# Products of a weight piece in another order in a hybrid decoder kernel: high halves first, remainders last

## The chip, the cores and the metric

The kernel runs on one core of a Trainium2 chip. The metric is the device time of one execution in microseconds (us), given as the median of several runs; less is better. The profile was taken on the chip in one further execution. Its engines are called PE (TensorE's matmuls; PEld is its weight loads), DVE (VectorE), ACT (ScalarE), POOL (GpSimd) and SP (SyncE, which issues most of the DMAs here).

## The reference

Two decoder layers over 256 tokens of width 2048, in float32. The first layer mixes tokens with latent attention, the second with a state-space scan; behind each mixer stands a dense MLP with a squared ReLU, and each part adds to the residual stream. The change lies in the MLP, which is computed twice:

```python
def squared_relu_mlp(h, w_in, w_out):
    u = jax.nn.relu(h @ w_in)
    return (u * u) @ w_out
...
        x = x + mix
        h = rms_norm(x, mlp_norm_g[i])
        x = x + squared_relu_mlp(h, mlp_w_in[i], mlp_w_out[i])
```

`w_in` is 2048 x 8192 and `w_out` 8192 x 2048, so each layer's MLP reads 134 MB of weights.

## The kernel before, in words

**Three products for one.** PE multiplies in a format with fewer bits than float32 (`F32R`). So each float32 operand is split in two: a high half, which is the value rounded to that format, and a remainder, which is the value less its high half. A product of `a` and `w` is summed from three: high a x high w, high a x remainder w, remainder a x high w. In the code the halves of the activations are `ah` and `al`, those of the weights `wh` and `wl`. The activations are the stationary operand (128 x 128, loaded by an instruction of its own, PEld), the weights the moving one (128 x 512). Each product is one matmul of 512 columns that adds to a PSUM bank.

**The flow of weights.** Weights come in units of 128 x 1024 float32, 512 KB. `Flow.next` (called at the head of `products` and, through `piece`, of `block`) keeps the flow ahead of PE: SP issues the DMAs of the units up to six ahead into the pool `raw` (6 buffers; some go to `rx`), and `convert` splits the units up to three ahead. The split of a unit is two instructions in `Flow.halves`: ACT copies the raw unit to its high half in a buffer of the pool `wh` (L102), then DVE subtracts that from the raw unit to give the remainder in a buffer of the pool `wl` (L103). Both pools have 4 buffers. A buffer can be written again when PE has run the last product that reads it.

**The MLP.** `mlp_body` walks over a list of tokens that `plan` writes out. A token is one unit of weights:

- `s` tokens belong to a scheme with seven block products in place of eight for `h @ w_in` (M1, N7, N5, N6, N4, M2, N3). Some of their units are sums of two pieces of weights, which DVE (L183) and DMAs that accumulate (POOL, L199) make. Such a unit goes to one PSUM bank (`st` in the trace, from the pools `acc` or `sm`) and has two halves of 512 columns, q = 0 and 1: six products.
- `c` tokens compute `h @ w_in` plainly (the first of eight column groups), `o` tokens `u @ w_out`. Their units go to two banks, one for each half of the tokens, t = 0 and 1: twelve products. An `o` block is four such units, 48 products, into the pair of banks of the pool `yp`; then `add_residual` (L436, DVE) adds first the bank t = 0 and then t = 1 to the residual stream. The next `o` block writes to the same pair of banks.

Between the blocks ACT and DVE evacuate the banks of the seven products (`after`: L620, L621 and others), and PE transposes the hidden values (L322, L324, to bank `sm`).

**The order of work.** PE runs its instructions in the order in which the program issues them (`manual_schedule`). In `products`, `self.flow.next(key)` stands first: what it issues on SP, ACT, DVE and POOL comes ahead of the unit's products. Lines L616 to L618 are the three products: L616 `ah x wh`, L617 `ah x wl`, L618 `al x wh`. The first `wl` product of a unit is its second product, and its last product reads `wh`.

**Where another order is in use.** `block` (L339, L340, L343), which computes the mixers' projections and the last part of each MLP, takes a unit in two passes: first all products with `wh` (L339 `ah`, L340 `al`, for both q and both t), then all with `wl` (L343).

Of the kernel before, what the change touches and what calls it, by code (L numbers as in the profile page):

```python
# [214 lines left out]
class Trunk:  # L215
# [343 lines left out]
    def mlp_body(self, mp, layer, gain):  # L559
        nc = self.nc  # L560
# [21 lines left out]
        def lhs_u(pp):  # L582
            return self.from_tiles([us[pp, 0], us[pp, 1]])
# [24 lines left out]

        def products(accs, key, lhs, kt, first, last):
            u, (h, lo) = self.flow.next(key)  # L610
            for q in range(2):
                k = 2 * kt + q
                wh, wl = h[:, q * 512:(q + 1) * 512], lo[:, q * 512:(q + 1) * 512]
                for t, b in enumerate(accs):
                    ah, al = lhs(k, t)
                    nc.tensor.matmul(b, ah, wh, start=first and q == 0, stop=False)  # L616
                    nc.tensor.matmul(b, ah, wl, start=False, stop=False)  # L617
                    nc.tensor.matmul(b, al, wh, start=False, stop=last and q == 1)  # L618

        sub = lambda o, a, b: nc.vector.tensor_tensor(o, a, b, ALU.subtract)  # L620
        plus = lambda o, a, b: nc.vector.tensor_tensor(o, a, b, ALU.add)  # L621
# [34 lines left out]
        for tok in tokens:  # L656
            key = (tok[0], layer) + tok[1:]
            if tok[0] == "s":
# [4 lines left out]
                if count.setdefault(name, 0) % 4 == 0:  # L663
                    pool = self.sm if name == "N7" else self.acc
                    bank[name] = pool.tile([P, 512], F32, tag=pool.name, name=self.name("st"))
                count[name] += 1
                products([bank[name]], key, lambda k, t: [x[:, k] for x in S[name]], d,
                         count[name] % 4 == 1, count[name] % 4 == 0)
                if count[name] % 4 == 0:
                    after(name, p)  # L670
                move(1.36)
            elif tok[0] == "c":
                _, p, j, o = tok
                if o == 0:
                    out["c"] = pair_of_banks(self.yp if j else self.acc)
                products(out["c"], key, lhs_x, o, o == 0, o == 7)
                if o == 7:
                    for t in range(2):
                        turn(relu(out["c"][t], t), p, j, t, TR[4])
                    if j:  # L680
                        when(3, steps[2])
                if o % 2:
                    self.tick()
                move(2.72)
            else:
                _, p, nb, o = tok
                if o == 0:
                    out[nb] = pair_of_banks(self.yp)
                products(out[nb], key, lhs_u(p), o, o == 0, o == 3)
                if o == 3:  # L690
                    self.add_residual(nb, out.pop(nb))
                move(2.72)
# [4 lines left out]
        for nb in range(4):  # L697
# [4 lines left out]
            accs = self.block(keys, lhs_u(7))  # L702
# [905 lines left out]
```

## Time and profile before

| | |
|---|---|
| median of 3 runs | 2285.71 us |
| lowest and highest run | 2285.32 and 2286.46 us |
| span of the profiled execution | 2284.5 us |
| first MLP, about | 272 to 970 us |
| second MLP, about | 1525 to 2270 us |
| products of L616 to L618 | 5424 |

The span runs from the first to the last instruction of the profiled execution; the time of a run has about 1.2 us more around it. In the profile, a line such as `L617 PE MATMUL st<-wl,xt ... x448 | 174.7, 390 | 0.0` is a group of instructions: line of the program, engine, operation, what it writes and reads by the program's names, how many, busy time in us, mean duration in ns, and the idle time of the engine just before them with what ended it. Matmuls are pipelined: one begins before the one ahead of it has ended, so busy times of PE are not a sum of steps. A row of the view of waits names the engine and line that waited, who ended the wait, the total in us, how many times, and the longest. A row of the timeline has the start and duration in us, engine, line, operation, tiles and count, and in brackets the idle time before it.

### The profile page before, as it was taken

To read this page: it belongs to the slowest core of one execution; us is meant where nothing else is said; L and a number is where in the kernel's file an instruction comes from. 1 tells how busy PE (TensorE), PEld (TensorE's weight loads), DVE (VectorE), ACT (ScalarE), POOL (GpSimd) and SP (SyncE) were. 2 spreads that over 40 slices of the span, in tenths; PEclk is the share of its full clock that TensorE was granted. 3 is DMA by queue.
4 is the path that set the end of the run, shared out by engine and by line. 5 is a ranking of instruction groups with operands and counts; after the bars stand their busy time and mean duration, and the time that the engine had idled before them with its cause. 6 is when DMAs were issued, how large, how long until landed. Compare 5 with 4: busy or idle time off the path is not lost.

```text
span 2284.5 us, 30768 instructions
## 1 busy us (share of the span) xinstructions
PE 2278.1 (100%) x10929; PEld 1889.6 (83%) x10929; DVE 1915.9 (84%) x2318; ACT 1390.1 (61%) x1947; POOL 275.5 (12%) x315
## 2 busy tenths in 40 slices
PE   9999999999999999999999999999999999999999
PEld 7898888888888888888888888888888888888887
DVE  7786698999898897687899688676989889989985
ACT  7775576566666666564666555545666666666663
POOL 1440000000000000100133213121000000000000
PEclk9999999999999999999999999999999999999999
DMA  8545678888888878667888787767688888888874
GB/s 315 173 153 159 211 230 267 259 255 270 264 255 259 267 232 271 227 208 241 277 280 278 245 275 264 229 222 229 204 265 248 259 270 253 260 275 247 267 232 160
DMA packets 167706, 557.16 MB, mean 244 GB/s; under 512 B 19040, under 2 KB 28192, under 8 KB 166528
## 3 DMA queue, kind: packets, MB, share of 16 engines
q1 hardware_dynamic: 151264, 502.44, 66.2%
q0 software_dynamic: 13888, 48.49, 10.0%
q10 hardware_dynamic: 2400, 4.27, 0.5%
q8 instruction: 86, 1.41, 0.3%
q14 instruction: 68, 0.56, 0.1%
HBM read 529.65 MB, written 6.41 MB: 235 GB/s over the span
## 4 chain that ended last, share of the span: by engine, by line
PE 96%; DVE 1%; DMA 1%; ACT 1%; issue 1%; POOL 0%; SPq 0%; ACTq 0%; DVEq 0%
PE acc L339 13%; PE acc L340 13%; PE acc L343 13%; PE yp L618 9%; PE yp L617 9%; PE yp L616 9%; PE st L617 7%; PE st L618 7%; PE st L616 7%; DMA wraw<-mi 1%; PE sm L324 1%; DVE wl L103 1%; PE y L1309 1%; PE sm L322 1%; PE acc L616 1%; PE acc L618 1%
## 5 line engine op out<-in xcount | busy, mean ns | idle before, releaser
L102 ACT ACTIVATE wh<-wraw 128x1024 fp32r<-128x1024 f32 (+1 forms) x818 | 856.2, 1053 | 570.4 <-PE acc L340 268.9
L103 DVE TENSOR_TENSOR wl<-wraw,wh 128x1024 fp32r<-128x1024 f32 (+1 forms) x818 | 985.5, 1221 | 240.6 <-ACT wh L102 216.6
L616 PE MATMUL yp<-wh,k 128*128 128x512 f32 x896 | 349.2, 390 | 0.0
L618 PE MATMUL yp<-wh,k 128*128 128x512 f32 x896 | 348.8, 389 | 0.0
L617 PE MATMUL yp<-wl,k 128*128 128x512 f32 x896 | 348.6, 389 | 0.0
L339 PE MATMUL acc<-wh,xt 128*128 128x512 f32 x704 | 279.7, 397 | 0.4 <-ACT wh L102 0.4
L340 PE MATMUL acc<-wh,xt 128*128 128x512 f32 x704 | 274.9, 390 | 0.1
L102 ACT ACTIVATE wh<-wrx 128x1024 fp32r<-128x1024 f32 x168 | 177.8, 1058 | 153.4 <-PE yp L618 101.7
L103 DVE TENSOR_TENSOR wl<-wrx,wh 128x1024 fp32r<-128x1024 f32 x168 | 204.3, 1221 | 36.6 <-ACT wh L102 35.6
L618 PEld LDWEIGHTS yp<-wh,k 128*128 128x128 f32 x896 | 168.2, 188 | 35.1
L617 PEld LDWEIGHTS yp<-wl,k 128*128 128x128 f32 x896 | 168.2, 188 | 34.9
L616 PEld LDWEIGHTS yp<-wh,k 128*128 128x128 f32 x896 | 168.2, 188 | 34.8
L339 PE MATMUL acc<-wh,k 128*128 128x512 f32 x496 | 196.5, 396 | 0.0
L340 PE MATMUL acc<-wh,k 128*128 128x512 f32 x496 | 193.3, 390 | 0.0
L343 PE MATMUL acc<-wl,xt 128*128 128x512 f32 x704 | 188.3, 389 | 0.0
L616 PE MATMUL st<-wh,xt 128*128 128x512 f32 x448 | 177.7, 397 | 0.0
L618 PE MATMUL st<-wh,xt 128*128 128x512 f32 x448 | 174.9, 390 | 0.0
L617 PE MATMUL st<-wl,xt 128*128 128x512 f32 x448 | 174.7, 390 | 0.0
L339 PEld LDWEIGHTS acc<-wh,xt 128*128 128x128 f32 x704 | 132.7, 188 | 29.4 <-ACT wh L102 1.6
L340 PEld LDWEIGHTS acc<-wh,xt 128*128 128x128 f32 x704 | 132.5, 188 | 28.5 <-issue 1.2
L343 PEld LDWEIGHTS acc<-wl,xt 128*128 128x128 f32 x704 | 132.1, 188 | 27.7
L199 POOL DMA_DIRECT2D wrx<-mi x56 | 49.2, 878 | 720.6 <-DVE wl L103 524.5
(318 smaller groups left out, 3527.0 us busy)
## 6 DMA issues: line engine op xcount, KB each, us to landing
wraw<-mi SPq DMA_DIRECT2D x256, 512.0 KB, 5.5
wraw<-mo SPq DMA_DIRECT2D x256, 512.0 KB, 5.6
wraw<-si SPq DMA_DIRECT2D x160, 512.0 KB, 5.2
wraw<-so SPq DMA_DIRECT2D x64, 512.0 KB, 5.2
wrx<-mi SPq DMA_DIRECT2D x56, 512.0 KB, 5.4
wrx<-mi POOLq DMA_DIRECT2D x56, 512.0 KB, 7.8
wraw<-wo SPq DMA_DIRECT2D x32, 512.0 KB, 4.0
taps<-xD SPq DMA_DIRECT2D x16, 768.0 KB, 8.4
```

Source lines behind the costliest of these rows:

```text
L102: self.last = nc.scalar.activation(h[:, v], raw[:, v], AF.Copy)
L103: self.last_lo = nc.vector.tensor_tensor(lo[:, v], raw[:, v], h[:, v].bitcast(F32), ALU.subtract)
L199: nc.gpsimd.dma_start(st["b11"].tile, quarter(d, 1, 0), accum_op=ALU.add)
L322: self.nc.tensor.transpose(b.bitcast(F32R)[:, v], words[:, v], self.ident_r)
L324: self.nc.tensor.transpose(b[:, v], src[:, v], self.ident)
L339: nc.tensor.matmul(accs[t][:, :n], ah, wh[:, q, :], start=first and kt + q == 0, stop=False)
L340: nc.tensor.matmul(accs[t][:, :n], al, wh[:, q, :], start=False, stop=False)
L343: nc.tensor.matmul(accs[t][:, :n], lhs(kt + q, t)[0], wl[:, q, :], start=False, stop=en and q == nk - 1)
L616: nc.tensor.matmul(b, ah, wh, start=first and q == 0, stop=False)
L617: nc.tensor.matmul(b, ah, wl, start=False, stop=False)
L618: nc.tensor.matmul(b, al, wh, start=False, stop=last and q == 1)
L1309: nc.tensor.matmul(y[t][c, o], part(t)[:, c], xg[g][t][:, o], start=True, stop=True)
```

## The change

Inside `products` the loops are parted. The old code ran for each half q and each bank t the three products L616, L617, L618 one after the other. The new code first runs, for both q and both t, the two products with the high half `h` of the weights, and then, in loops of their own, those with the remainder `lo`. The flags that open a bank's sum (`start`) stay with the first product of a bank; those that close it (`stop`) move from the last product with `al` to the last with `lo`. Nothing else is touched: the number of products, their operands, the flow's buffers, the tokens and their order stay.

```diff
         def products(accs, key, lhs, kt, first, last):
             u, (h, lo) = self.flow.next(key)
+            half = lambda w, q: w[:, q * 512:(q + 1) * 512]
             for q in range(2):
-                k = 2 * kt + q
-                wh, wl = h[:, q * 512:(q + 1) * 512], lo[:, q * 512:(q + 1) * 512]
                 for t, b in enumerate(accs):
-                    ah, al = lhs(k, t)
-                    nc.tensor.matmul(b, ah, wh, start=first and q == 0, stop=False)
-                    nc.tensor.matmul(b, ah, wl, start=False, stop=False)
-                    nc.tensor.matmul(b, al, wh, start=False, stop=last and q == 1)
+                    ah, al = lhs(2 * kt + q, t)
+                    nc.tensor.matmul(b, ah, half(h, q), start=first and q == 0, stop=False)
+                    nc.tensor.matmul(b, al, half(h, q), start=False, stop=False)
+            for q in range(2):
+                for t, b in enumerate(accs):
+                    nc.tensor.matmul(b, lhs(2 * kt + q, t)[0], half(lo, q), start=False, stop=last and q == 1)
```

For a unit with one bank the order of the six products changes from h, lo, h, h, lo, h to h, h, h, h, lo, lo. For a unit with two banks the twelve go from (h, lo, h) four times, three to a bank, to eight with h, two to a bank in turn, and then four with lo, one to a bank in turn.

## The prediction

> **What bounds the kernel now.** I read the page's head and its chain of waits first, to find the engine whose time is the span.
>
> ```profile
> span 2284.5 us, 30768 instructions
> ...
> PE 2278.1 (100%) x10929; PEld 1889.6 (83%) x10929; DVE 1915.9 (84%) x2318; ACT 1390.1 (61%) x1947; POOL 275.5 (12%) x315
> ...
> PEclk9999999999999999999999999999999999999999
> ...
> PE 96%; DVE 1%; DMA 1%; ACT 1%; issue 1%; POOL 0%; SPq 0%; ACTq 0%; DVEq 0%
> ```
>
> The chain that ended last is 96% PE, and the granted clock never falls. So the time is a sum of products, and a change of order can only gain where PE stands still. Next I asked who made PE wait. A product is a weight load (PEld) and a matmul (PE); where the load waits for data, PE stands. The view of waits, for the loads, from the start of the first MLP to the end of the second (columns: us in all, times, longest):
>
> ```profile
> PEld st L617 <- DVE wl L103: 3.2, 8, 0.5
> ...
> PEld yp L617 <- DVE wl L103: 0.5, 2, 0.3
> ```
>
> Ten times L617, the product with the remainder `wl`, waited for VectorE to make it, 3.7 us together. L616 and L618, the products with the high half `wh`, have no row. This is the only idle time that the changed lines have to give: 0.16% of the span. What a wait costs is read from the steps from one start to the next in PE's timeline. First undisturbed ones, from a `block` of the second mixer:
>
> ```profile
> 1303.08 1.07 PE L343 MATMUL acc<-wl,xt 128*128 128x512 f32 x4
> 1303.98 0.39 PE L339 MATMUL acc<-wh,xt 128*128 128x512 f32 x1
> ...
> 1306.70 0.39 PE L339 MATMUL acc<-wh,xt 128*128 128x512 f32 x1
> ```
>
> From 1303.98 to 1306.70 run the twelve products of one piece: 2.72 us, a step of 0.227, while each "lasts" 0.39, since a product overlaps the next. Now the longest of the ten waits:
>
> ```profile
> 569.32 0.39 PE L618 MATMUL st<-wh,sN 128*128 128x512 f32 x1
> 569.55 0.40 PE L616 MATMUL st<-wh,sN 128*128 128x512 f32 x1
> 570.01 0.50 PE L617 MATMUL st<-wl,sN 128*128 128x512 f32 x1
> 570.35 0.40 PE L618 MATMUL st<-wh,sN 128*128 128x512 f32 x1
> ```
>
> From 569.55 to 570.35 two steps took 0.80 us instead of 0.454: this wait of 0.50 cost 0.35. The 0.15 between them is what a load can be late without delaying the product before it.
>
> **The change part by part.** It keeps the number of products and sorts them. A one-bank unit (bank `st`) has six; the old order is, for each half-piece q, high, remainder, high; the new one four with `wh`, then two with `wl`. A two-bank unit (blocks "c" and "o") has twelve; new: eight with `wh`, then four with `wl`. The groups by line give the counts:
>
> ```profile
> L617 PE MATMUL yp<-wl,k 128*128 128x512 f32 x896 | 348.6, 389 | 0.0
> ...
> L343 PE MATMUL acc<-wl,xt 128*128 128x512 f32 x704 | 188.3, 389 | 0.0
> ...
> L617 PE MATMUL st<-wl,xt 128*128 128x512 f32 x448 | 174.7, 390 | 0.0
> ...
> L617 PE MATMUL st<-wl,sN 128*128 128x512 f32 x336 | 131.5, 391 | 0.3
> ...
> L617 PE MATMUL yp<-wl,xt 128*128 128x512 f32 x64 | 25.1, 392 | 0.0
> ...
> L617 PE MATMUL acc<-wl,xt 128*128 128x512 f32 x64 | 24.9, 389 | 0.0
> ```
>
> 1808 remainder products move: 784 in one-bank units and 1024 in two-bank units. No instruction is added or removed; every other queue gets its work as before, since `flow.next`, which issues conversions and loads, stands ahead of the products in both orders.
>
> *The products themselves: 0.* The old order used one stationary operand twice running (`ah` with `wh`, then with `wl`); the new one doesn't. That loses no saved load: the page counts 10929 loads for 10929 products. The new order of a two-bank unit is already run by `block` (L339, L340, then L343), so its speed can be read off the timeline above: four remainder products that alternate between two banks took 0.90 us, from 1303.08 to 1303.98, four plain steps. The groups agree: 389 ns for L343, 389 to 392 for L617. Rounding of these means leaves ±0.5 ns on each of the 1024 products that now alternate: ±0.5 us. I take 0.
>
> [...]
>
> *The ten waits: minus 2.2 us.* Each costs its idle time less the 0.15 that a load has to spare: 3.7 - 10 x 0.15 = 2.2 us. In the new order the first `wl` product is three steps later in a one-bank unit (0.68 us) and seven later in a two-bank unit (1.59 us). The longest wait was 0.50, so each of the ten is covered. In the unit shown, which starts at 569.55, the remainder would be wanted at 569.55 + 4 x 0.227 = 570.46; it was ready at 570.01. What is late next: nothing that has a row. The units behind start up to 0.35 us earlier, and their own remainders are wanted 0.68 to 1.59 us later than now.
>
> *Release of the buffers: 0.* The last `wh` product moves from the 6th to the 4th place, or from the 12th to the 8th: its buffer comes free 0.45 or 0.91 us earlier. The last `wl` product moves from the 5th to the 6th, or 11th to 12th: 0.23 us later. Who waits for these buffers, in the whole kernel:
>
> ```profile
> ACT wh L102 <- PE yp L618: 260.3, 172, 1.7
> DVE wl L103 <- ACT wh L102: 252.2, 247, 3.7
> ...
> ACT wh L102 <- PE st L618: 71.0, 250, 0.3
> ```
>
> ACT waits for the last high product of a unit (L618) and VectorE for ACT; VectorE has no row in which it waits for a remainder's buffer. Both would therefore run earlier. PE doesn't wait for them except the ten times above, so this is cover, not time.
>
> *Evacuation of the first bank: 0, covered.* In a two-bank unit the first bank's last product moves from the 9th to the 11th place, 0.45 us later; the second bank's stays last. Its reader at the end of an "o" block is `add_residual` on VectorE (L436):
>
> ```profile
> 761.11 0.39 PE L617 MATMUL yp<-wl,k 128*128 128x512 f32 x1
> ...
> 761.27 1.28 DVE L436 TENSOR_TENSOR x<-yp,x 128x512 f32<-128x512 f32 x2
> 761.33 0.39 PE L618 MATMUL yp<-wh,k 128*128 128x512 f32 x1
> ...
> 761.76 1.06 ACT L102 ACTIVATE wh<-wraw 128x1024 fp32r<-128x1024 f32 x1 [1.66 <-PE yp L618]
> ...
> 763.57 1.23 DVE L183 TENSOR_TENSOR wraw<-wraw,wraw 128x1024 f32<-128x1024 f32 x1 [1.01 <-DMA wraw<-mi]
> ...
> 764.28 0.39 PE L616 MATMUL yp<-wh,k 128*128 128x512 f32 x1
> ```
>
> The first add began at 761.27, while the block's last product, of the other bank, began at 761.33. Now the first bank ends with the product in the slot of 761.11, at 761.50; ACT started 0.04 after the product it waited for, so the add starts at about 761.54, 0.27 us late. Queued behind it are the second add and VectorE's next piece. Here both fit: VectorE idled 1.01 us after them, and the bank's next writer starts at 764.28. If that cover were gone, it would cost 0.27 us for each block (second rival). The "c" blocks' `relu` on ACT shifts likewise, but there are only two a layer. The row of 761.76 also shows what hides the later release of `wl`: between the release of the high buffer and VectorE's use of the other stands ACT's conversion, 1.06 us.
>
> Sum: -2.2 us. The profiled execution spans 2284.5, 1.2 under the median of the runs, 2285.7 (what lies around the span); the same difference on both sides gives a span of 2282.3 and a time of **2283.5 us**, -0.1%.
>
> **The rivals.**
>
> *The waits stay.* VectorE's lateness may be more than the ten waits show, and the waits move to the new `wl` place. For it: VectorE is the engine with least room. Stretches of the two MLPs:
>
> ```profile
> 272.00:970.00 698.00, 697.83 (x3168) 576.22 (x3167) 616.69 (x615) 437.94 (x487) 45.47 (x67) 1.00 0.82 254
> 1525.00:2270.00 745.00, 744.90 (x3429) 614.74 (x3428) 645.24 (x642) 456.65 (x504) 50.04 (x67) 1.00 0.80 246
> ```
>
> (columns: length, then busy time of PE, PEld, DVE, ACT, POOL.) VectorE is busy 88% and 87%. Against it: it has 81 and 100 us free, and the longest wait is 0.50 against 0.68 of new room. Time: 2285.7.
>
> *VectorE pays for the later bank (the other side).* Place: L436 behind each "o" block. Price 0.27 us a block:
>
> ```profile
> L436 DVE TENSOR_TENSOR x<-yp,x x112: 679/682/687, 352.8 to 2237.2; 128x512 f32<-128x512 f32 x112
> ```
>
> 112 adds are 56 blocks, so at most 56 x 0.27 = 15.1 us, with the ten waits unremoved: 2300.8. It decides where the work behind the add has less than 0.27 us to spare even after its remainder's later place. For it: the 88%. Against it: the 1.01 us of idle in the block shown, and the 0.68 to 1.59 us that the pieces gain.
>
> *The step behind a transpose shrinks too (faster).* Where a unit follows a transpose, its first step is long:
>
> ```profile
> 568.02 0.30 PE L324 MATMUL sm<-ident,s 128*128 128x128 f32 x1
> ...
> 568.08 0.48 PE L616 MATMUL st<-wh,sN 128*128 128x512 f32 x1
> ...
> 568.39 0.40 PE L617 MATMUL st<-wl,sN 128*128 128x512 f32 x1
> ```
>
> 0.31 instead of 0.227. If this were the second product's wait for `wl`, the new order would end it. The transposes to bank `sm` bound their number:
>
> ```profile
> L324 PE MATMUL sm<-ident,s 128*128 128x128 f32 x167 | 33.7, 281 | 0.0
> L322 PE MATMUL sm<-ident,tr 128*128 128x128 f32 x229 | 26.9, 236 | 0.0
> ```
>
> Four to a group, at most 99 places, 0.083 us each: 8.2 us, with the ten waits 2275.3. Against it: the `block` order has the same long step behind short products:
>
> ```profile
> 1301.13 0.50 PE L339 MATMUL acc<-wh,xt 128*128 128x512 f32 x1
> 1301.47 0.39 PE L340 MATMUL acc<-wh,xt 128*128 128x512 f32 x1
> ```
>
> [...]
>
> **How the numbers follow.** The forecast has 0.78; the waits stay 0.10; the transposes 0.04; VectorE pays 0.06; the banks 0.02. A measurement of this kernel can tell about 0.2% from no change, 4.6 us: 2281.1 to 2290.3 is "the same". Forecast and first rival lie inside: same 0.88, faster 0.04, slower 0.08. Range: below, the whole 3.7 us of idle is gained instead of 2.2, with the runs' scatter (2285.32, 0.4 under the median) and the 0.5 of rounding: 2281.1. Above, nothing is gained, with the scatter on that side (2286.46, 0.75) and the 0.5: 2287.0. The rivals outside it hold 0.12.
>
> **What would show it.** Right: no row of a load waiting for `wl` within the MLPs; four high products, then two (or eight, then four) at 0.227 us a step; PE's busy time as now; ACT's waits for PE's high products end earlier. Wrong: a row of L436 waiting for PE together with a new wait of PE (second rival); a granted clock below 1.00, or remainder products over 0.227 us apart (banks); short steps behind transposes. The forecast would also fail if VectorE or ACT ran their instructions in another order than now.

## The result, and the profile after

| | before | after |
|---|---|---|
| median | 2285.71 us | 2303.01 us |
| lowest and highest | 2285.32 and 2286.46 us | 2300.80 and 2305.64 us |
| profiled execution | span 2284.5 us | 2305.32 us, span 2303.5 us |

The ratio of after to before is 1.0077, with an interval of 1.0065 to 1.009: the kernel is 0.8% slower, 17 us, where 2.2 us less were forecast. Of the kernels in the experiments below, e1 and e6 had one run each, of 6050 and 3260 us, far off all others; these two are left out of the ratios. The change shifted the lines behind it: the products are now L615 (`ah x wh`), L616 (`al x wh`) and L619 (`ah x wl`), while L103, L183 and L436 are as before.

The head of the page of after:

```profile
span 2303.5 us, 31032 instructions
...
PE 2284.5 (99%) x10929; PEld 1891.2 (82%) x10929; DVE 1914.7 (83%) x2318; ACT 1389.4 (60%) x1947; POOL 275.2 (12%) x315
```

Each engine's count of busy instructions is the same as before (the 264 more in the head are of kinds that the page doesn't count as busy), and so is DVE's busy time (1914.7 against 1915.9). PE is 19 us short of the span now; before it was 6.4 short. So no engine got more work: PE stands still. For whom, the view of waits tells (us in all, times, longest):

```profile
DVE wraw L183 <- DMA wraw<-mi: 37.1, 18, 4.5
...
DVE x L436 <- PE yp L619: 15.7, 28, 1.1
...
PE yp L615 <- DVE x L436: 11.5, 9, 3.0
```

Before, PE had no row in which it waited for L436, and the first row read:

```profile
DVE wraw L183 <- DMA wraw<-mi: 18.1, 27, 2.0
```

PE waits for `add_residual`, the add that empties its bank. And L183, the sum that makes the unit N7 from two raw pieces, waits longer for the DMA of its second piece, although the same DMAs are issued. The view of waits for the weight loads, from the start of the first MLP to the end of the second, still shows what the forecast was about:

```profile
PEld yp L615 <- ACT wh L102: 4.3, 3, 1.6
...
PEld st L619 <- DVE wl L103: 0.8, 2, 0.5
```

Of the ten waits for the remainder `wl`, 3.7 us together, two with 0.8 us are left. That gain is there, and something larger stands on top of it. The first row is a part of that: its three loads stand ahead of the first product of a block, where PE waits for L436. ACT had been done for 0.2 to 0.5 us when these loads began (at the first it ended at 515.25, the load began at 515.63), so the add ended these waits too.

**One block in both traces.** DVE's timeline of before at the end of an "o" block (start, duration, engine, line, tiles, count, idle time ahead):

```profile
676.54 1.23 DVE L103 TENSOR_TENSOR wl<-wraw,wh 128x1024 fp32r<-128x1024 f32 x1
677.68 1.28 DVE L436 TENSOR_TENSOR x<-yp,x 128x512 f32<-128x512 f32 x2
679.41 1.23 DVE L183 TENSOR_TENSOR wraw<-wraw,wraw 128x1024 f32<-128x1024 f32 x1 [0.44 <-DMA wraw<-mi]
```

The two adds come first, then the sum, which waits 0.44 us for its DMA with nothing urgent behind it. The same place after:

```profile
678.85 1.23 DVE L103 TENSOR_TENSOR wl<-wraw,wh 128x1024 fp32r<-128x1024 f32 x1
684.56 1.23 DVE L183 TENSOR_TENSOR wraw<-wraw,wraw 128x1024 f32<-128x1024 f32 x1 [4.48 <-DMA wraw<-mi]
685.70 1.28 DVE L436 TENSOR_TENSOR x<-yp,x 128x512 f32<-128x512 f32 x2
686.90 2.35 DVE L103 TENSOR_TENSOR wl<-wraw,wh 128x1024 fp32r<-128x1024 f32 x2
```

The sum now stands ahead of the adds. DVE runs its queue in order, as the rows show: for 4.48 us it waits for the DMA while two full banks wait for it. Not all of the 4.48 comes from the swap. The two adds take 1.2 us, by which the sum now comes earlier; but the DMA too took longer here, 7.8 us from issue to landing (676.66 to 684.44) against 5.5 before (673.76 to 679.28). Why it did, no run here shows. PE's timeline there:

```profile
682.95 0.61 PE L619 MATMUL st<-wl,sN 128*128 128x512 f32 x2
686.53 0.47 PE L615 MATMUL yp<-wh,k 128*128 128x512 f32 x1 [2.97 <-DVE x L436]
...
687.48 0.63 PE L616 MATMUL yp<-wh,k 128*128 128x512 f32 x1
687.91 0.63 PE L615 MATMUL yp<-wh,k 128*128 128x512 f32 x1
688.33 0.63 PE L616 MATMUL yp<-wh,k 128*128 128x512 f32 x1
```

The next "o" block's first product starts 0.83 us behind the start of the adds. A microsecond later the steps are 0.42 to 0.43 us instead of 0.227, and the granted clock is lower: 0.61 from 686.40 to 690.40, against 1.00 in the stretch before. The windows of both (length, busy time of PE, PEld, DVE, ACT and POOL with counts, granted clock, share of the DMA engines, GB/s):

```profile
683.00:686.40 3.40, 0.56 (x3) 0.14 (x1) 1.84 (x3) 1.06 (x1) 0.00 (x0) 1.00 1.01 278
686.40:690.40 4.00, 3.87 (x10) 2.96 (x11) 4.00 (x5) 0.55 (x1) 0.00 (x0) 0.61 0.54 133
```

**Who moved the sum.** In the program's text nothing on DVE changed place. But only PE's order is written out by hand; DVE's and ACT's queues are ordered when the program is compiled. The instruction order of the two compiled programs can be compared, buffer by buffer: 157 of DVE's 2318 instructions and 95 of ACT's stand elsewhere, none of SP's or POOL's. DVE's order at one block, before:

```
L103 wl_4368
L436 x_142<-yp_4246
L436 x_146<-yp_4247
L183 wraw_4399<-wraw_4397,wraw_4399
L103 wl_4388
```

and after:

```
L103 wl_4368
L183 wraw_4399<-wraw_4397,wraw_4399
L436 x_142<-yp_4246
L436 x_146<-yp_4247
L103 wl_4388
```

At ten "o" blocks, five in each MLP, each the first block of its pair of columns, the sum for N7 moved ahead of both adds in this way. At these ten the sum waited 9.0 us for its DMA before and 26.8 after.

**The account.** From the trace one can take, for each 512-column product in the two MLPs, the step from its start to the next start, less the plain 0.2267 us, and add these up. It gives 12.3 us before and 31.2 us after: 18.9 more, against 19.0 more of span. Of the 31.2, the pauses ahead of the ten blocks are 13.2 us (one of 3.13, two of 2.1 to 2.5, three of 1.0 to 1.4, four of 0.2 to 0.7), and 22 products behind three of them, at a granted clock of 0.50 and steps of about 0.427 us, 22 x 0.2 = 4.4 us. The other steps hold 13.6 us, 1.3 more than before: about 1.6 less in waits for `wl` (2.2 before, 0.5 after), about 3 more in small ones. 1.8 of these 3 are steps of 0.30 to 0.34 us at the head of the ten blocks, two or three behind each pause.

### The profile page after: what moved, and what is told of

The parts are those of the page before. It is cut to its first block, busy times and chain, and to the rows that moved or that the text cites. A ratio compares the mean times of both kernels' runs of the same rounds, so it can differ in the third digit from the quotient of the medians.

```text
span 2303.5 us, 31032 instructions
## 1 busy us (share of the span) xinstructions
PE 2284.5 (99%) x10929; PEld 1891.2 (82%) x10929; DVE 1914.7 (83%) x2318; ACT 1389.4 (60%) x1947; POOL 275.2 (12%) x315
## 4 chain that ended last, share of the span: by engine, by line
PE 95%; DVE 2%; DMA 2%; issue 1%; ACT 0%; POOL 0%; DVEq 0%; SPq 0%; ACTq 0%
PE acc L339 13%; PE acc L340 13%; PE acc L343 13%; PE yp L615 9%; PE yp L619 9%; PE yp L616 9%; PE st L615 7%; PE st L619 7%; PE st L616 7%; DMA wraw<-mi 1%; DVE wl L103 1%; PE sm L324 1%; PE sm L322 1%; PE y L1310 1%; PE acc L615 1%
## 5 line engine op out<-in xcount | busy, mean ns | idle before, releaser
L103 DVE TENSOR_TENSOR wl<-wraw,wh 128x1024 fp32r<-128x1024 f32 (+1 forms) x818 | 984.8, 1222 | 236.9 <-ACT wh L102 218.9
L615 PE MATMUL yp<-wh,k 128*128 128x512 f32 x896 | 352.4, 393 | 11.6 <-DVE x L436 11.5
L616 PE MATMUL yp<-wh,k 128*128 128x512 f32 x896 | 350.7, 391 | 0.0
L619 PE MATMUL yp<-wl,k 128*128 128x512 f32 x896 | 241.7, 392 | 0.0
L103 DVE TENSOR_TENSOR wl<-wrx,wh 128x1024 fp32r<-128x1024 f32 x168 | 204.5, 1222 | 25.6 <-ACT wh L102 24.5
L615 PEld LDWEIGHTS yp<-wh,k 128*128 128x128 f32 x896 | 169.1, 189 | 52.6 <-issue 11.3
L619 PEld LDWEIGHTS yp<-wl,k 128*128 128x128 f32 x896 | 169.8, 190 | 35.8
L616 PEld LDWEIGHTS yp<-wh,k 128*128 128x128 f32 x896 | 169.1, 189 | 34.5
L343 PE MATMUL acc<-wl,xt 128*128 128x512 f32 x704 | 188.3, 389 | 0.0
L615 PE MATMUL st<-wh,xt 128*128 128x512 f32 x448 | 177.7, 397 | 0.0
L616 PE MATMUL st<-wh,xt 128*128 128x512 f32 x448 | 174.8, 390 | 0.0
L343 PEld LDWEIGHTS acc<-wl,xt 128*128 128x128 f32 x704 | 132.1, 188 | 27.7
L619 PE MATMUL st<-wl,xt 128*128 128x512 f32 x448 | 138.1, 389 | 0.0
```

Source lines behind the costliest of these rows:

```text
L103: self.last_lo = nc.vector.tensor_tensor(lo[:, v], raw[:, v], h[:, v].bitcast(F32), ALU.subtract)
L343: nc.tensor.matmul(accs[t][:, :n], lhs(kt + q, t)[0], wl[:, q, :], start=False, stop=en and q == nk - 1)
L615: nc.tensor.matmul(b, ah, half(h, q), start=first and q == 0, stop=False)
L616: nc.tensor.matmul(b, al, half(h, q), start=False, stop=False)
L619: nc.tensor.matmul(b, lhs(2 * kt + q, t)[0], half(lo, q), start=False, stop=last and q == 1)
```

## The experiments

The theory to be tested: the loss is the ten swaps in DVE's queue, and without them the change brings what was forecast. Its rivals: the later end of the first bank costs by itself, the new product order does (banks in turn), or only one kind of unit is to blame. Times are medians; the ratios are to the kernel before on the same chip, 2286.65 us for the first four kernels and 2286.30 us on another chip for the last three. The last column is the sum of steps over 0.2267 us as above.

| kernel | median, us | ratio, interval | span of the profile | steps over 0.2267 |
|---|---|---|---|---|
| before (first profile) | 2285.71 | | 2284.5 | 12.3 |
| after (first profile) | 2303.01 | 1.0077, 1.0065 to 1.009 | 2303.5 | 31.2 |
| e1: after, sum held behind the adds | 2284.10 | 0.999, 0.998 to 0.9999 | 2282.3 | 10.1 |
| e2: old products, sum first | 2301.08 | 1.0067, 1.005 to 1.0084 | 2300.0 | 28.0 |
| e3: new order in one-bank units only | 2297.62 | 1.0046, 1.0031 to 1.0061 | 2296.4 | 23.8 |
| e4: new order in two-bank units only | 2304.29 | 1.0079, 1.0064 to 1.0094 | 2303.0 | 31.1 |
| e6: e3, sum held | 2285.67 | 0.9999, 0.9989 to 1.0008 | 2285.6 | 11.5 |
| e7: e4, sum held | 2286.20 | 1.0, 0.999 to 1.0009 | 2283.4 | 11.2 |
| e8: after, all sums held | 2284.81 | 0.9995, 0.9986 to 1.0005 | 2282.8 | 10.9 |

### e1: the changed kernel with the sum held behind the adds

The products stay as changed. `add_residual` keeps its last add, and N7's sum is told to be issued behind it:

```diff
             if name == "N7":
-                add("b22", "b12", "b22")
+                with flow.tc.issue_after(flow.add.ins) if flow.add else nullcontext():
+                    add("b22", "b12", "b22")
...
-            self.nc.vector.tensor_tensor(x, accs[t], x, ALU.add)
+            self.flow.add = self.nc.vector.tensor_tensor(x, accs[t], x, ALU.add)
```

> The new product order, with one thing held: the sum for N7 (L183, b22) may not stand ahead of the add_residual (L436) that the program wrote before it, in VectorE's queue. Theory A (the ten places where that sum, which waits for its DMA, went ahead of the two adds cost the time): PE's waits of up to 3.0 us for the bank of an 'o' block vanish, no product runs at the 0.427 us step behind them, and the time is 2282 to 2286 us. Theory B (the new product order itself, or the rest of the moved work on VectorE and ACT, costs it): the time stays at 2300 or above. Between 2287 and 2299: both have a share, to be read as the difference from 2284 and from 2303.

Measured: 2284.10 us, 19 us less than after, and 2.55 under the kernel before on the same chip, with an interval that just excludes no change. It is faster than both kernels, than the one before by little. ACT's order is that of after, so ACT's 95 moved instructions cost nothing by themselves.

DVE's timeline at the block that was shown above (L104 makes the remainders here, L184 is the sum, L438 the adds, L618, L619 and L622 the products):

```profile
675.77 1.23 DVE L104 TENSOR_TENSOR wl<-wraw,wh 128x1024 fp32r<-128x1024 f32 x1
677.57 1.29 DVE L438 TENSOR_TENSOR x<-yp,x 128x512 f32<-128x512 f32 x2 [0.58 <-PE yp L622]
678.78 2.35 DVE L104 TENSOR_TENSOR wl<-wraw,wh 128x1024 fp32r<-128x1024 f32 x2
...
682.30 1.22 DVE L184 TENSOR_TENSOR wraw<-wraw,wraw 128x1024 f32<-128x1024 f32 x1
```

The adds run as soon as the bank is full, and the sum, now behind three remainders as well, finds its data there and waits for nothing. The view of waits agrees:

```profile
DVE x L438 <- PE yp L622: 22.8, 40, 1.1
...
DVE wraw L184 <- DMA wraw<-mi: 3.3, 4, 1.1
```

The first row is the later end of the first bank: 40 times DVE waits for it, 0.57 us each. PE has no row for L438 at all. So that lateness is real and costs nothing.

### e2: the old products with the sum first

The kernel before, in which ten sums, those at the ten blocks, are put ahead of the adds by an order between them; ten DVE rows stand elsewhere than before, no row of ACT.

```diff
-                add("b22", "b12", "b22")
+                total = add("b22", "b12", "b22")
+                if p in range(2, 7) and flow.adds and flow.done - flow.adds[0] <= 4:
+                    for ins in flow.adds[1:]:
+                        flow.tc.add_manual_dep(ins, total.ins.name, mybir.DependencyInfo(
+                            mybir.DependencyClass.NoSync, mybir.DependencyReason.DATA), reason="sum first")
...
-            self.nc.vector.tensor_tensor(x, accs[t], x, ALU.add)
+            ins = self.nc.vector.tensor_tensor(x, accs[t], x, ALU.add).ins
+            self.flow.adds = ([self.flow.done] if t == 0 else self.flow.adds) + [ins] if nb == 0 else None
```

> The old product order, with ten instructions moved in VectorE's queue: at the same ten 'o' blocks the sum for N7 (L183) is put ahead of the two adds. Theory A: the loss comes back without any change of the products: waits of PE for the bank at these ten blocks, 2297 to 2306 us. Theory B (product order): 2285 to 2287 us.

Measured: 2301.08 us. No product has moved against the kernel before, and most of the loss is there: 15.7 us of steps over 0.2267, against 18.9 after. From its view of waits and from its DVE timeline (L442 are the adds, L624 the products `ah x wh`):

```profile
PE yp L624 <- DVE x L442: 10.4, 9, 2.3
```

```profile
510.37 1.23 DVE L104 TENSOR_TENSOR wl<-wraw,wh 128x1024 fp32r<-128x1024 f32 x1
514.98 1.23 DVE L184 TENSOR_TENSOR wraw<-wraw,wraw 128x1024 f32<-128x1024 f32 x1 [3.38 <-DMA wraw<-mi]
516.12 1.28 DVE L442 TENSOR_TENSOR x<-yp,x 128x512 f32<-128x512 f32 x2
```

It is the picture of after: the sum waits for its DMA, the adds behind it, PE behind the adds. The ten swaps alone bring most of the loss, and with them taken out (e1) nothing of it is left.

### e3 and e4: the new order in one kind of unit only

In e3 units with one bank run the new loops and those with two banks the old ones; in e4 it is the other way round.

```diff
             u, (h, lo) = self.flow.next(key)
+            if len(accs) == 1:
...
+            else:
...
```

> The new order in the six-product units (one bank) alone, the old one in the twelve-product units. VectorE's queue then has the sum ahead of the adds at two of the ten blocks (the second 'o' block group of the second column pair in each layer), which cost 0.5 and 0.6 us in the changed kernel. Theory A: eight of the ten waits for a remainder are gone (-1.9 us) and about 1 us is lost at the two blocks: 2284 to 2287 us. Theory B: the 1568 moved products of these units cost their share, about 784 of 1808 of 17 us: about 2293 us.

> The new order in the twelve-product units (two banks) alone, the old one in the six-product units. VectorE's queue has the sum ahead of the adds at all ten blocks. Theory A: nearly the whole loss, 2297 to 2306 us, with waits of PE for the bank at the ten blocks. Theory B: the share of these units, about 1024 of 1808 of 17 us: about 2295 us.

e3 was expected near the kernel before and took 2297.62 us: a miss. Its order on DVE explains it. At two of the ten blocks the sum stands ahead of both adds, at the other eight between the two. DVE's timeline at one of the eight, and the row of waits:

```profile
513.45 0.69 DVE L436 TENSOR_TENSOR x<-yp,x 128x512 f32<-128x512 f32 x1 [0.17 <-PE yp L629]
516.55 1.23 DVE L183 TENSOR_TENSOR wraw<-wraw,wraw 128x1024 f32<-128x1024 f32 x1 [2.40 <-DMA wraw<-mi]
517.69 0.68 DVE L436 TENSOR_TENSOR x<-yp,x 128x512 f32<-128x512 f32 x1
```

```profile
PE yp L627 <- DVE x L436: 7.2, 9, 1.2
```

The first add escapes and PE can start the next block with the first bank; it stops at the second. Each pause is shorter, 1.2 us at most, and the loss is 11.5 us of steps. So even the part of the change that leaves the "o" blocks' own products alone reorders DVE around them.

e4 took 2304.29 us, like after. All ten pauses stand ahead of a block's first product:

```profile
PE yp L616 <- DVE x L436: 13.0, 10, 2.1
```

### e6 and e7: the same two, with the sum held

e6 is e3 and e7 is e4, each with the edit of e1.

> The kernel with the new order in the six-product units alone, now with the sum for N7 held behind both adds. Theory A (where the sum stands among the adds is the whole loss; in the kernel without the hold it stood between the two adds at eight blocks and ahead of both at two): the 11 us go, and of the ten waits for a remainder the eight in these units go too: 2283.5 to 2286 us. Theory B (the new order of these units costs time by itself): it stays above 2290 us.

> The kernel with the new order in the twelve-product units alone, with the sum for N7 held behind both adds. Theory A: the 18 us go; the eight waits for a remainder in the six-product units stay as in the kernel before: 2285 to 2287 us. Theory B (the later first bank, or the alternating banks, cost time by themselves): above 2290 us.

Measured: 2285.67 us and 2286.20 us; neither differs from the kernel before. So neither part of the product order costs anything that these runs can tell (the intervals reach about 0.1%), the two-bank part with its banks in turn included. The gain isn't seen in either alone. In e6, where eight of the ten waits for `wl` should have gone, waits for remainders stand elsewhere (e6's profiled run was one of two at 2287.3 us; seven others lay between 2285.1 and 2286.1):

```profile
PEld acc L345 <- DVE wl L104: 1.8, 1, 1.8
PEld yp L631 <- DVE wl L104: 1.7, 4, 0.6
```

In e7 DVE waits for the later first bank 20 times, with no row of PE waiting for L438, and the one-bank units keep their old order and four of their waits, where eight were expected:

```profile
DVE x L438 <- PE yp L623: 8.9, 20, 1.1
...
PEld st L631 <- DVE wl L104: 1.7, 4, 0.9
```

### e8: all sums behind the adds

The hold of e1, put around every sum of two pieces (N7, N5 and N6), to see whether more is to be had.

> The new product order with every sum of weight pieces (L183: N7, N5, N6) held behind the add_residual written before it, not the N7 sums alone. If only sums that wait for a DMA do harm ahead of the adds, this changes nothing against the run that held the N7 sums alone: 2283 to 2285 us. If the other sums that the changed kernel moved ahead of adds at eight blocks cost something too, it is faster than that by up to 8 x 0.5 us: 2280 us. If holding them makes remainders late, a wait for a remainder shows and it is slower, 2285 to 2290 us.

Measured: 2284.81 us, 1.5 under the kernel before, with an interval that holds no change. Nothing is gained over e1. The text above takes other sums to have been moved ahead of adds in after. Against the kernel before, only the ten N7 sums were; the others that this run holds back stood ahead of their adds in both.

Not tried: a larger pool of raw buffers, with which the sum's DMA might land earlier. Not settled: by which rule the compiler's ordering chose. That the first bank now fills two products later, so that by the compiler's estimate the sum is ready before the adds, is an argument. It fits that the sum stands ahead of both adds at all ten blocks in e4 and after, where that bank fills later, and between them at eight of ten in e3, where it doesn't; no run shows more.

## Why the prediction was wrong

**The step that failed** is the sentence "every other queue gets its work as before, since `flow.next` ... stands ahead of the products in both orders". It holds for the program's text, and for SP and POOL in the compiled program; DVE and ACT were reordered. On it rested *Evacuation of the first bank: 0, covered*: "VectorE idled 1.01 us after them". That idle time was the sum waiting for its DMA right behind the adds, read as cover. It was the danger: the same instruction, one place further ahead, holds the adds for as long as the DMA is late. The text named another order on DVE or ACT among the things that would make it fail, and gave it no chance and no price. A price could have been read: L183 waited for its DMA 18.1 us in all before, up to 2.0 at a time, and 9.0 of them right behind the adds of the ten blocks. That would have been rough: in after 26.8 us stand there, and the pauses of PE are 13.2.

**The products themselves, 0:** right. e1 runs the whole new order, and the group of its remainder products that alternate between two banks reads

```profile
L622 PE MATMUL yp<-wl,k 128*128 128x512 f32 x896 | 239.7, 389 | 0.0
```

389 ns, as L343's. In after the same group, L619, has 392, since it holds the products behind the three longest pauses, where the granted clock fell to 0.50: the four of a unit took 1.57, 1.91 and 1.76 us there, and 1.07 at a clock of 1.00.

**The ten waits, minus 2.2 us:** right once the swaps are out, the size too: by its steps, the ten waits cost 2.18 us in the kernel before. The span of e1 is 2282.3 us, as forecast, and its steps over 0.2267 sum to 10.1 against 12.3. In its view of waits for the loads two are left:

```profile
PEld st L622 <- DVE wl L104: 0.4, 2, 0.3
```

The interval of e1's ratio, 0.998 to 0.9999, leaves 0.2 to 4.6 us for the gain.

**Release of the buffers, 0:** nothing in e1, e7 or e8 speaks against it. With half of the change, e6, waits for `wl` turned up at other places, which the step didn't consider.

**VectorE pays for the later bank** (2300.8): its time came within 2.2 us of the result by luck; its mechanism isn't what happened. DVE does wait for the later bank, 28 times in after and 40 times in e1, and longer than the 0.27 us said; in e1 this costs PE nothing. The pauses are at ten blocks and not 56, and up to 3.13 us long. The sign that the prediction gave for this rival, a row of L436 waiting for PE together with a new wait of PE, did stand in after, so that sign didn't tell the rival from the swap; only e1 did.

**The waits stay** (2285.7): no; 0.8 us of 3.7 are left in after, 0.4 in e1.

**The step behind a transpose shrinks:** no. The unit of the longest wait, in e1's PE timeline:

```profile
568.04 0.48 PE L618 MATMUL st<-wh,sN 128*128 128x512 f32 x1
568.36 0.40 PE L619 MATMUL st<-wh,sN 128*128 128x512 f32 x1
...
569.52 0.40 PE L618 MATMUL st<-wh,sN 128*128 128x512 f32 x1
...
570.90 0.39 PE L618 MATMUL yp<-wh,k 128*128 128x512 f32 x1
```

Two products with `wh` instead of one with `wh` and one with `wl`, and the first step is still 0.32. The next unit, from 569.52, takes its six steps in 1.38 us without a wait, where one of 0.50 stood before.

**The banks** (0.02 among the chances): no run shows that products which go to two banks in turn run slower. In e1 such products with the remainder take 389 ns, as above, and e1 and e7, which run them, took 2284.10 and 2286.20 us at a granted clock of 1.00. In after the clock did fall, to 0.50 at three places in the MLPs, each behind a pause of PE.

## What to carry to other kernels

Where only one engine's order is fixed by hand and the others' queues are ordered at compile time, a reorder of the first can reorder the rest (here 157 instructions of DVE and 95 of ACT); compare the compiled queues, and not only the program's text. Look at what stands next to the instruction that empties a PSUM bank: a neighbour that waits for a DMA is no slack, since one swap can hand its wait to the bank and from there to PE (here the sum's waits at the ten blocks were 26.8 us after the swap, and the pauses of PE 13.2). Where such an order matters, state it in the program, as e1 does with one line.

## What the runs showed of the hardware

In after the granted clock fell behind the three longest of the ten pauses ahead of the "o" blocks, 3.36, 2.67 and 2.33 us from start to start. It fell from 1.00 to 0.50 at 687.25, 1861.43 and 2032.10, which is 0.7 to 1.2 us after PE had begun again, and seven or eight products ran at steps of about 0.427 us instead of 0.227. Behind the other seven pauses, of 1.57 us and less, it stayed at 1.00. In e4 it fell behind a pause of 2.15 us from start to start, in PE's timeline

```profile
2113.51 0.39 PE L629 MATMUL st<-wh,sN 128*128 128x512 f32 x1
2115.66 0.47 PE L616 MATMUL yp<-wh,k 128*128 128x512 f32 x1 [1.76 <-DVE x L436]
...
2118.20 1.91 PE L620 MATMUL yp<-wl,k 128*128 128x512 f32 x4
2119.91 0.63 PE L616 MATMUL yp<-wh,k 128*128 128x512 f32 x1
```

and not behind a longer one of 2.53:

```profile
1858.97 0.39 PE L629 MATMUL st<-wh,sN 128*128 128x512 f32 x1
1861.50 0.47 PE L616 MATMUL yp<-wh,k 128*128 128x512 f32 x1 [2.14 <-DVE x L436]
...
1863.49 1.07 PE L620 MATMUL yp<-wl,k 128*128 128x512 f32 x4
1864.40 0.39 PE L616 MATMUL yp<-wh,k 128*128 128x512 f32 x1
```

Four products (L620) took 1.71 us behind the pause of 2.15, and 0.91 us behind the pause of 2.53. The windows of the two stretches (columns as above; the granted clock stands behind POOL):

```profile
2115.60:2120.00 4.40, 4.33 (x13) 3.32 (x14) 4.40 (x5) 1.06 (x1) 0.00 (x0) 0.66 0.82 250
1861.50:1866.00 4.50, 4.50 (x20) 3.58 (x21) 4.50 (x5) 1.06 (x1) 0.00 (x0) 1.00 0.62 190
```

So the length of the pause alone doesn't decide here; what does is left open.

The drops are also a part of why after scatters more than before, 2300.80 to 2305.64 us: each of the three in its profile costs seven or eight times 0.2, about 1.5 us, and the spans of its runs are 2299.0 and 2300.7 us where the mean granted clock was 1.000, and 2301.2 to 2303.8 where it was 0.999 or 0.998. The pauses themselves vary as well: e3's four runs, all at 1.000, lie between 2293.42 and 2298.19 us.
